# A hybrid decoder step on one core: the gate's sample rows read turned from DRAM, the pool's last rows turned at the end, and another ending for the last two tiles

## The chip, the cores and the metric

The kernel runs on one core of a Trainium2 chip. Its work is issued on five engines with a queue each: TensorE (PE in the profile; PEld are its weight loads), VectorE (DVE), ScalarE (ACT), GpSimd (POOL) and SyncE (SP, which only issues DMAs). The metric is the device time of one execution in microseconds; lower is better.

## The reference, cut to what matters

One layer for a prompt of 1024 tokens and 8 sample tokens, 1024 channels, all in float32:

```python
xn = _rmsnorm(h, pre_g); proj = xn @ w_in
u, v, z_a, x_b, z_b, g_a, g_b = split(proj)
y_a = gelu(u) * spatial_mix(layernorm(gelu(v))) * silu(z_a)
pooled, new_pool = _pool_branch(x_b, prev_pool)     # windows of 2/4/8/16 tokens; new_pool: last 15 rows of x_b
y_b = pooled * silu(z_b)
m = sigmoid(g_a) * (y_a @ w_pa) + sigmoid(g_b) * (y_b @ w_pb)
h = h + _rmsnorm(m @ w_out, post_g)
e = p @ w_ple
gate = sigmoid(_rmsnorm(h, ple_in_g) @ w_pg)
h = h + _rmsnorm(gate * e, ple_out_g)
```

Outputs are `h` of the prompt and of the samples, the normalised `v` of the last chunk, and the pooling rows: the prompt's last 15 rows of `x_b`, and for each sample 14 rows of its old buffer and its new row.

## The kernel before, in words

Prompt and samples stand together as 1032 columns. A product of 1024 x 1024 by 1024 x 1032 is done by pairs of 128 output rows; a pair is one round of Strassen's scheme with seven products, P1 to P7 (`strassen`), each of 12 matmuls of 512 columns or 24 of 260. Each float32 operand is cut into a high and a low part (`split`: a copy on ScalarE, a difference on VectorE) and three of the four cross products are taken, in the form of one pass. A `Step` holds one product: what prepares its weights, the matmuls, and what takes the result out of PSUM; functions are hung behind a step with `at(step, f)`.

The stages in order of time: embedding product and the first branch (to about 400 us), the pooling branch with `XB`, `ZB` and `mixes` (about 360 to 560 us), the second gate, the two merged products, the output product (`Out`, with tokens on partitions) and the gate's product (`Embed`, `gatesteps`, four pairs of token tiles; the last pair holds tiles 6 and 7).

Every instruction is first collected by `Planner.take` with a guessed duration, then `Planner.order` writes out each engine's queue: of what can start, it takes what is due first (`late`, worked back from the uses; a TensorE product is due at its place in the plan's clock, `at`). Loads into the 46 general slots may start some 14 us ahead of their due time. At most eight DMAs of SP and ScalarE are let out at once. The chip then runs these queues as they were written, each engine waiting at the head of its queue. All instructions are issued in `play`, so the profile puts nearly all of them on line 301 and they are told apart by their tiles' names.

Names that the change touches. `XB.tails`: behind a pair of the pooling branch, TensorE turns the last 128 columns of two row blocks into the bank `tail`, ScalarE copies 32 rows of it into `big`, and behind the last pair two DMAs write the pooling outputs. `mixes(g)`: the pooling weights, loaded six steps and cut three steps ahead of their product by the common rule. `sample_stationary`: turns 8 rows into 128-row blocks with eight small transposes (bank `psst`) and VectorE takes them out, with a gain; used for the samples' embedding (`psamp`) and for the samples' rows at the gate (`hs`, in `gate_input(S)`). `sample_rows` and `sample_product`: the samples' product with the raw rows of a weight, four matmuls side by side, bank `sps`. `gated`: sigmoid, product with `e`, sum of squares, and for the last two tiles the product with the gain. `gate_finish`: root of the mean square (VectorE `ms`, GpSimd `rstd`), the scaling, the sum with `h`, the write. For tiles 6 and 7 that sum is one VectorE instruction for each half, with `h` loaded back as `hback`.

The last pair's seven products run in the order `LAST`: P1, P6, P7, P5, P4, P3, P2. P5 and P4 finish tile 7's two halves, P3 tile 6's second half, and P2, in two pieces of 256 columns (`last`), tile 6's first.

Of the kernel before, what the change touches and what calls it, by code (L numbers as in the profile page):

```python
# [19 lines left out]
NS = 8  # L20
# [6 lines left out]
EPS = 1e-6  # L27
POOL_BUF = 15
WINDOWS = (2, 4, 8, 16)
PLE = 256  # L30
# [25 lines left out]
class Planner:  # L56
# [8 lines left out]
    LOAD, LEAD, PATIENCE, RATE, SPARE = 14.0, 14.0, 60.0, 0.36, 3  # L65
    SPARED = 1.0

    def __init__(self, nc, slots, queues):
        self.nc, self.slots, self.queues = nc, slots, queues
        self.ops, self.seen, self.users, self.tags = [], {}, {}, {}  # L70
        self.fixed, self.open, self.clock = True, None, 0.0

        self.loose = set()
        for e in self.ENGINES:
            setattr(self, e, Taker(self, e))
# [54 lines left out]
    def duration(self, engine, method, out, reads, kwargs):  # L130
        n = out.free_size()
        if engine == "tensor":
            if method == "transpose":
                return 0.109
            return 0.3 if "tile_position" in kwargs else max(0.06, 0.0062 + n / 2268)
        if engine == "vector":
# [11 lines left out]
    def take(self, engine, method, args, kwargs):  # L148
# [11 lines left out]
        self.open = (name, op) if engine == "tensor" else None  # L160
        op.calls.append((method, args, kwargs))
        op.spent.append(op.busy)
# [12 lines left out]
        for ap in reads:  # L175
            self.touch(op, ap, False)
        for ap in writes:
            self.touch(op, ap, True)

    def apart(self):  # L180
# [127 lines left out]
def hybrid_step(  # L308
# [519 lines left out]
    def sample_sums(ps):  # L828
# [6 lines left out]
        return parts[2], parts[1]  # L835

    def sample_stationary(src, nk, gain=None):

# [253 lines left out]
    wgcut = {what: dram.tile([HALF, D], F32, tag="wg" + what, name="wg" + what) for what in ('T4', 'B22')}  # L1092
    kept["rowsum"] = dram.tile([NB, P], F32, tag="rowsum", name="rowsum")
    kept["wgleft"] = dram.tile([D, HALF], F32, tag="wgleft", name="wgleft")
# [88 lines left out]

    state_sb, tail = big[:, 7, :D], big[:, 6, :D]
    past = cpool.tile([P, NB, NS], F32, tag="past", name="past")
# [54 lines left out]
    def mixes(g):  # L1240
# [12 lines left out]
        for m in range(2):  # L1253
# [18 lines left out]

            steps.append(Step(nothing if m else prepare, run, evacuate))
        steps[0].loads = loads
        return steps

# [48 lines left out]
    for g, ((w, u), (wz, z)) in enumerate(zip(pairs_of(XB0, XB, "xb"), pairs_of(ZB0, ZB, "zb"))):  # L1325
        bsteps.append((strassen(w, xop, u), strassen(wz, xop, z), mixes(g)))
        xusers.append(u)
# [177 lines left out]
    def out_finish(t):  # L1505
# [6 lines left out]
        dma(kept["h"][t * P : t * P + r, :], h)  # L1512

    rin = lambda t: vsums[: rows(t), t, :1]

# [52 lines left out]
    def ge_start(t):  # L1568
        ge[t], e_of[t], parts[t] = slot("ge", (P, D)), slot("eback", (P, D)), []
        dma(e_of[t][: rows(t)], kept["e"][t * P : t * P + rows(t), :])  # L1570

    def gated(t, c, src):
# [4 lines left out]
        parts[t].append(square_here(g, e_of[t][:r, c]) if len(parts[t]) == 2 else square_sum(g, r))  # L1577
        if len(parts[t]) > 2:
            a, b = parts[t][:2]
            both = sm("both")  # L1580
            nc.vector.tensor_scalar(out=both[:r], in0=a[:r], scalar1=b[:r], scalar2=None, op0=ALU.add)
            parts[t][:2] = [both]
        if NB - 2 <= t < NB:
            mul(g, g, gains["out"][:r, c])

    def gate_finish(t):
        r = rows(t)
        rs = rstd(parts.pop(t), r)
        g = ge.pop(t)
        del e_of[t]  # L1590
        if not NB - 2 <= t < NB:
            g = g[:r]
            nc.vector.scalar_tensor_tensor(out=g, in0=g, scalar=rs[:r], in1=gains["out"][:r],
                                           op0=ALU.mult, op1=ALU.mult)
            nc.gpsimd.dma_start(out=g, in_=kept["h"][t * P : t * P + r, :], accum_op=ALU.add)
            dma(y_of(t), g)
            return
        h = slot("hback", (P, D))
        dma(h, kept["h"][t * P : (t + 1) * P, :])
        for j in range(2):  # L1600
            nc.vector.scalar_tensor_tensor(out=g[:, half(j)], in0=g[:, half(j)], scalar=rs,
                                           in1=h[:, half(j)], op0=ALU.mult, op1=ALU.add)
            dma(y_of(t)[:, half(j)], g[:, half(j)])

    class Embed(User):
        def loads(self):
            for m in range(2):
                ge_start(2 * self.pair + m)

        def direct(self, m, j, ps, c=None):  # L1610
            gated(2 * self.pair + m, c or half(j), ps)

        def summed(self, m, j, ps, u, free=None):
# [3 lines left out]
            gated(t, half(j), o)  # L1617
            if len(parts[t]) == 2:
                gate_finish(t)

        def finish(self):
            for m in range(2):
                if 2 * self.pair + m in ge:
# [299 lines left out]
```

## Time and profile before

| what | value |
|---|---|
| runs | 976.0, 977.59, 977.63 us; median 977.59 |
| profiled execution | 975.89 us, its span 973.8 us |
| granted TensorE clock | 0.997 |
| TensorE busy | 963.8 us, 6077 matmuls |
| VectorE busy | 799.4 us, 1266 instructions |
| ScalarE busy | 532.8 us, 898 instructions |
| GpSimd busy | 68.9 us, 141 instructions |
| DMA | 119308 packets, 185.56 MB |

A timeline row gives the start, the duration, the engine, the line, the operation, output and inputs by their names, the shape and a count. Starts are in us from the beginning of the span. The row of a group gives the shortest, median and longest duration in ns, and the first and last start. A row of windows gives for each engine the busy time in that stretch, then the granted clock, the busy share of the DMA engines and GB/s.

### The profile page before, as it was taken

Reading aid. Unit: us, or ns where it says so; the run is one execution under the profiler, and the core shown is the slowest. Engines: PE = TensorE matmul, PEld = TensorE weight load, DVE = VectorE, ACT = ScalarE, POOL = GpSimd, SP = SyncE. Lnnn points to the kernel's source line nnn. Section 1 sums busy time; section 2 is a strip of 40 time slices with the busy share of each in tenths; the row PEclk is TensorE's granted clock in tenths of the full one; section 3 lists DMA queues with packets and bytes.
Section 4 is the critical chain, followed back from the end, with each engine's and each line's share of the span. In section 5 each row is a group of like instructions: output and inputs, shape, how many; then the busy total and the mean of one; then the engine's idle time right before and its main releaser. Section 6 shows DMA issues by size and latency. Waiting matters only on the chain. (4 is left out here: it accounts for less than half of the span.)

```text
span 973.8 us, 16071 instructions
## 1 busy us (share of the span) xinstructions
PE 963.8 (99%) x6077; PEld 858.9 (88%) x6077; DVE 799.4 (82%) x1266; ACT 532.8 (55%) x898; POOL 68.9 (7%) x141
## 2 busy tenths in 40 slices
PE   9999999999999999999999999999999999999996
PEld 6889999999999999999999999999999986888775
DVE  6997568786889688979897987697699799769786
ACT  7966899865444433344442343552353263977662
POOL 1200000000000000000000100000000001312222
PEclk9999999999999999999999999999999999999998
DMA  9545752532373353666735076884583393799966
GB/s 324 194 130 131 153 153 87 197 104 70 131 281 130 121 185 100 246 218 203 259 122 194 17 257 222 288 301 152 185 294 109 137 339 100 170 280 362 291 187 196
DMA packets 119308, 185.56 MB, mean 191 GB/s; under 512 B 29183, under 2 KB 75735, under 8 KB 119222
## 3 DMA queue, kind: packets, MB, share of 16 engines
q1 hardware_dynamic: 117102, 177.11, 54.1%
q0 software_dynamic: 2080, 7.41, 4.3%
q8 instruction: 48, 0.79, 0.3%
q14 instruction: 30, 0.25, 0.1%
q10 hardware_dynamic: 48, 0.01, 0.0%
HBM read 125.85 MB, written 53.87 MB: 185 GB/s over the span
## 5 line engine op out<-in xcount | busy, mean ns | idle before, releaser
L301 DVE TENSOR_TENSOR u<-acc,u 128x520 f32<-128x520 f32 (+1 forms) x84 | 58.3, 694 | 24.5 <-PE acc L301 22.6
L301 POOL TENSOR_TENSOR rstd<-ms,mhalf 128x1 f32<-128x1 f32 (+1 forms) x36 | 30.4, 885 | 228.2 <-DVE ms L301 196.3
L301 POOL MEMSET u<- 128x8 f32 x32 | 3.3, 104 | 491.1 <-PE acc L301 210.6
L301 ACT ACTIVATE u<-acc 128x512 f32<-128x512 f32 x36 | 21.4, 595 | 23.4 <-PE acc L301 22.7
L301 ACT ACTIVATE paw<-pas 128x512 fp32r<-128x512 f32 x16 | 10.0, 628 | 30.3 <-DVE pas L301 25.1
L301 ACT ACTIVATE pbw<-pbs 128x512 fp32r<-128x512 f32 x16 | 10.0, 628 | 28.9 <-DVE pbs L301 25.7
L301 DVE TENSOR_TENSOR v<-acc,v 128x520 f32<-128x520 f32 (+1 forms) x20 | 13.8, 692 | 12.7 <-PE acc L301 12.6
L301 ACT ACT_TABLE_LOAD x17 | 21.8, 1283 | 4.5 <-PE acc L301 2.0
L301 DVE TENSOR_TENSOR big<-big 128x1024 f32<-128x1024 f32 (+4 forms) x20 | 23.7, 1215 | 0.0
L301 ACT ACTIVATE big<-v 128x1024 uint16<-128x1024 uint16 x16 | 18.6, 1171 | 6.9 <-DMA v<-vw 6.9
L301 PE MATMUL accm<-qh,wpoolw 128*128 128x260 f32 (+1 forms) x96 | 20.9, 320 | 0.0
L301 ACT ACTIVATE zbw<-zbs 128x512 fp32r<-128x512 f32 x16 | 10.0, 627 | 16.5 <-DVE zbs L301 12.3
L301 ACT ACTIVATE big<-mix 128x256 f32<-128x256 f32 x32 | 11.7, 378 | 13.1 <-PE mix L301 12.7
L301 DVE TENSOR_TENSOR acc<-acc,u 128x512 f32<-128x512 f32 (+1 forms) x16 | 11.1, 697 | 8.7 <-PE acc L301 8.7
L301 ACT ACTIVATE gbw<-gbs 128x512 fp32r<-128x512 f32 x16 | 10.0, 626 | 14.8 <-DVE gbs L301 12.6
L301 ACT ACTIVATE uw<-us 128x512 fp32r<-128x512 f32 x16 | 10.0, 627 | 14.0 <-DVE us L301 6.8
L301 PEld LDWEIGHTS accm<-qh,wpoolw 128*128 128x128 f32 x96 | 15.6, 188 | 1.9
L301 ACT ACTIVATE zaw<-zas 128x512 fp32r<-128x512 f32 x16 | 10.1, 629 | 13.1 <-PE acc L301 5.2
L301 DVE TENSOR_TENSOR big<-mix,big 128x256 f32<-128x256 f32 x32 | 12.7, 419 | 5.5 <-ACT big L301 5.3
L301 ACT ACTIVATE vw<-v 128x1024 uint16<-128x1024 uint16 x16 | 16.2, 1044 | 1.8 <-DVE v L301 1.8
L301 ACT ACTIVATE u<-u 128x1032 f32<-128x1032 f32 (+1 forms) x8 | 6.8, 852 | 18.9 <-DVE u L301 18.8
L301 ACT ACTIVATE gb<-gb 128x1032 f32<-128x1032 f32 (+1 forms) x8 | 6.8, 854 | 18.5 <-DVE gb L301 18.5
(668 smaller groups left out, 3593.9 us busy)
## 6 DMA issues: line engine op xcount, KB each, us to landing
ga<-ga SPq DMA_DIRECT2D x16, 516.0 KB
gb<-gb SPq DMA_DIRECT2D x16, 516.0 KB
vraw<-in_w_in_dram SPq DMA_DIRECT2D x22, 256.0 KB
ya<-za SPq DMA_DIRECT2D x8, 516.0 KB
yb<-zb SPq DMA_DIRECT2D x8, 516.0 KB
x<-in_x_prompt_dram SPq DMA_DIRECT2D x8, 512.0 KB
e<-e SPq DMA_DIRECT2D x8, 512.0 KB
garaw<-in_w_in_dram SPq DMA_DIRECT2D x8, 512.0 KB
```

Source lines behind the costliest of these rows:

```text
L301: getattr(getattr(self.nc, e), method)(*args, **kwargs)
```

## The change

Four parts. First, the pooling branch's last columns are no longer turned behind each pair: each row block writes its last 23 columns (15 of the prompt, 8 samples) as they are into a DRAM tensor `ends`; at the end of the kernel one load brings them back, TensorE turns the eight blocks, ScalarE copies two halves out, and two DMAs on ScalarE's queue write the outputs. Second, the samples' rows for the gate are read from DRAM in turned form, element by element, by one DMA on ScalarE's queue; the uses of them move five steps later. Third, the pooling weights' load and cut hang behind fixed steps. Fourth, the ending of tiles 6 and 7: for tile 6's first half, gain times `e` and `e` squared are prepared ahead, so that behind the sigmoid stand a square on ScalarE, a weighted sum on VectorE and one product; its second half gets its gain after the last sum. Tile 7's first half is scaled and added on TensorE (the identity times `h`, a scaled identity times the gate) and copied out and written by ScalarE. The planner gets what it needs for this: a landing time by pieces, a fourfold price for a float32 matmul of 512 columns, and `behind`, which holds an instruction back behind another.

```diff
 class Planner:
-    SPARED = 1.0
+    SPARED, PACKET = 1.0, 0.0025
...
+            if self.packets:
+                op.lands = 2.0 + self.packets * self.PACKET
...
+    def words(out, in_):
+        plan.packets = out.size()
+        dma(out, in_, nc.scalar)
+        plan.packets = 0
...
+    def sample_turned(src, nk, gain=None):
+        turned, st = past.rearrange("p b t -> p (b t)")[:, : NS * nk], twice[:, : nk * NS].rearrange("p (k s) -> p k s", k=nk)
+        words(turned, src.rearrange("s (k p) -> p (s k)", p=P))
+        turned = turned.rearrange("p (s k) -> p k s", k=nk)
...
+            mul(st, turned, gain.unsqueeze(2).to_broadcast([P, nk, NS]))
+        return st
...
         def tails(self):
-            ps = bank("tail")
-            b = 2 * self.pair
             for i in range(2):
-                nc.tensor.transpose(ps[:, i * P : (i + 1) * P], self.out[i][:, T - P : T], ident)
-            nc.scalar.activation(out=tail[96:P, b * P : (b + 2) * P], in_=ps[96:P, : 2 * P], func=AF.Copy)
-            if b == NB - 2:
-                dma(o_pool[0, 0], tail[P - NS - POOL_BUF : P - NS, :])
-                dma(o_spool[0, :, POOL_BUF - 1, :], tail[P - NS : P, :])
+                b = 2 * self.pair + i
+                dma(kept["ends"][b * P : (b + 1) * P, :], self.out[i][:, SEQ - POOL_BUF : T])
...
+        mix, load, prepare = mixes(g)
+        bsteps.append((strassen(w, xop, u), strassen(wz, xop, z), mix))
+        at(bsteps[g][1][1], load)
+        at(bsteps[g][1][5], prepare)
...
         if t == S:
-            samples["h"] = sample_stationary(got, NB, gvec[:, 2 * NB :])
+            samples["h"] = sample_turned(kept["h"][SEQ:T, :], NB, gvec[:, 2 * NB :])
             return
...
+    def gate_ahead():
+        e, c = e_of[END], slice(0, HALF)
+        both = slot("eahead", (P, 2, HALF))
+        mul(both[:, 0], e[:, c], e[:, c])
+        mul(both[:, 1], e[:, c], gains["out"][:, c])
+        ahead["square"], ahead["gain"], ahead["root"] = both[:, 0], both[:, 1], slot("sahead", (P, HALF))
...
+        if t == END and c.start < HALF:
+            s, square = sm("ssq"), ahead["root"][:, c]
+            nc.scalar.activation(out=square, in_=g, func=AF.Square)
+            ahead["squared"] = plan.ops[-1]
+            nc.vector.scalar_tensor_tensor(out=square, in0=square, scalar=1.0 / D, in1=ahead["square"][:, c],
+                                           op0=ALU.mult, op1=ALU.mult, accum_out=s)
+            ahead["summed", c.start] = plan.ops[-1]
+            mul(g, g, ahead["gain"][:, c])
+            ahead["ready", c.start] = plan.ops[-1]
...
+    def last_sum(t, c, rs, h):
+        g = ge[t][:, c]
+        nc.vector.scalar_tensor_tensor(out=g, in0=g, scalar=rs, in1=h[:, c], op0=ALU.mult, op1=ALU.add)
+        dma(y_of(t)[:, c], g)
+
+    def pool_rows():
+        ends, o, ps = slot("ends", (P, NB, ENDS)), slot("rows", (P, D)), region("ends")
+        dma(ends, kept["ends"].rearrange("(b p) t -> p b t", p=P))
+        for b in range(NB):
+            nc.tensor.transpose(ps[:ENDS, b // 4, b % 4 * P : (b % 4 + 1) * P], ends[:, b], ident)
+        plan.ops[-1].at += 8.0
         for j in range(2):
...
+            nc.scalar.activation(out=o[:ENDS, half(j)], in_=ps[:ENDS, j], func=AF.Copy)
+        dma(o_pool[0, 0], o[:POOL_BUF], nc.scalar)
+        dma(o_spool[0, :, POOL_BUF - 1, :], o[POOL_BUF:ENDS], nc.scalar)
+
+    def last_finish():
...
+        t, h = END + 1, hs[END + 1]
+        rs = rstd(parts.pop(t))
+        with plan.behind(ahead["ready", 0]):
+            last_sum(t, half(1), rs, h)
+        scaled, ps, o = slot("scaled", (P, P)), bank("final"), slot("final", (P, HALF))
+        with plan.behind(ahead["squared"]):
+            nc.scalar.activation(out=scaled, in_=ident, func=AF.Copy, scale=rs)
+        for w, x in ((ident, h), (scaled, ge[t])):
+            plan.apart()
+            nc.tensor.matmul(ps, w, x[:, :HALF], start=w is ident, stop=w is scaled)
+            plan.ops[-1].at += 12.0
+        pool_rows()
+        nc.scalar.activation(out=o, in_=ps, func=AF.Copy)
+        dma(y_of(t)[:, :HALF], o, nc.scalar)
+        t, h = END, hs[END]
+        with plan.behind(ahead["summed", QUART]):
+            mul(ge[t][:, half(1)], ge[t][:, half(1)], gains["out"][:, half(1)])
+        rs = rstd(parts.pop(t))
+        for c in (half(1), *CUTS):
+            last_sum(t, c, rs, h)
...
-    at(outsteps[2][3], lambda: gate_input(S))
-    at(gatesteps[0][4], lambda: sample_rows("wg", w_pg, 0))
-    at(gatesteps[1][1], lambda: sample_product("wg", samples["h"], 0))
-    at(gatesteps[1][1], lambda: sample_rows("wg", w_pg, 1))
-    at(gatesteps[1][5], lambda: sample_product("wg", samples["h"], 1))
-    at(gatesteps[1][5], embed_gate_sample)
+    at(gatesteps[0][0], lambda: gate_input(S))
+    at(gatesteps[1][2], lambda: sample_rows("wg", w_pg, 0))
+    at(gatesteps[1][6], lambda: sample_product("wg", samples["h"], 0))
+    at(gatesteps[1][6], lambda: sample_rows("wg", w_pg, 1))
+    at(gatesteps[2][3], lambda: sample_product("wg", samples["h"], 1))
+    at(gatesteps[2][3], embed_gate_sample)
```

More of the change, by code (lines that the diff above doesn't have):

```diff
@@ L161, in take @@
         op.calls.append((method, args, kwargs))
+        if self.first:
+            op.before.add(self.first)
         op.spent.append(op.busy)
@@ L178, in take, with behind @@
             self.touch(op, ap, True)
+    @contextmanager
+    def behind(self, op):
+        self.first = op
+        yield
+        self.first = None
     def apart(self):
@@ L835, in sample_sums @@
         return parts[2], parts[1]
+    def sample_turned(src, nk, gain=None):
+        turned, st = past.rearrange("p b t -> p (b t)")[:, : NS * nk], twice[:, : nk * NS].rearrange("p (k s) -> p k s", k=nk)
+        words(turned, src.rearrange("s (k p) -> p (s k)", p=P))
+        turned = turned.rearrange("p (s k) -> p k s", k=nk)
+        if gain is None:
+            nc.vector.tensor_copy(out=st, in_=turned)
+        else:
+            mul(st, turned, gain.unsqueeze(2).to_broadcast([P, nk, NS]))
+        return st
     def sample_stationary(src, nk, gain=None):
@@ L1271, in evacuate @@
                                                    op0=ALU.mult, op1=ALU.mult)
-            steps.append(Step(nothing if m else prepare, run, evacuate))
-        steps[0].loads = loads
-        return steps
+            steps.append(Step(nothing, run, evacuate))
+        return steps, loads, prepare
     class Merge(User):
@@ L1575, in gated @@
         nc.scalar.activation(out=g, in_=src, func=AF.Sigmoid, scale=rin(t))
-        mul(g, e_of[t][:r, c], g)
[L1577 to L1583, printed above, removed]
+        if t == END and c.start < HALF:
[7 more added lines that the diff above has]
+            ahead["ready", c.start] = plan.ops[-1]
+            parts[t].append(s)
+            if c.start == 0:
+                a, b = parts[t]
+                both = sm("both")
+                nc.vector.tensor_scalar(out=both, in0=a, scalar1=b, scalar2=None, op0=ALU.add)
+                parts[t] = [both]
+            return
+        mul(g, e_of[t][:r, c], g)
+        parts[t].append(square_sum(g, r))
+        if t == NB - 1:
             mul(g, g, gains["out"][:r, c])
@@ L1590, in gate_finish @@
         del e_of[t]
[L1591 to L1599, printed above, removed]
-        for j in range(2):
-            nc.vector.scalar_tensor_tensor(out=g[:, half(j)], in0=g[:, half(j)], scalar=rs,
-                                           in1=h[:, half(j)], op0=ALU.mult, op1=ALU.add)
-            dma(y_of(t)[:, half(j)], g[:, half(j)])
+        g = g[:r]
@@ L1617, in summed @@
             gated(t, half(j), o)
-            if len(parts[t]) == 2:
+            if len(parts[t]) == 2 and t < END:
                 gate_finish(t)
         def finish(self):
+            if self.pair == NPAIR - 1:
+                last_finish()
+                return
             for m in range(2):
```

26 lines of the change are left out of this document (20 added, 6 removed).

## The prediction

> **What bounds the kernel now.** I read the engine totals first, then TensorE's order of time around the transposes that the change touches, then the last ten microseconds engine by engine. In the totals (busy us, share of the span, instructions):
>
> ```profile
> span 973.8 us, 16071 instructions
> PE 963.8 (99%) x6077; PEld 858.9 (88%) x6077; DVE 799.4 (82%) x1266; ACT 532.8 (55%) x898; POOL 68.9 (7%) x141
> ```
>
> TensorE is idle for 10.0 us. The end of the kernel takes 8.4 of them, as the rows below show, so before the last product it hardly ever waits. What leaves TensorE's queue ahead of that product therefore comes off the time, one for one, as long as nothing else becomes late. What leaves VectorE or ScalarE there saves nothing.
>
> TensorE in order of time, at the sample transposes and at the first pair of tail transposes (start, duration, instruction):
>
> ```profile
> 849.14 0.39 PE L301 MATMUL acct<-woT3l,mw 128*128 128x512 f32 x1
> 849.37 0.39 PE L301 MATMUL acct<-woT3h,mw 128*128 128x512 f32 x1
> 849.69 0.66 PE L301 MATMUL psst<-ident,hs 8*128 8x8 f32 x8
> 850.28 0.50 PE L301 MATMUL acct<-woT4h,mw 128*128 128x512 f32 x1
> 850.62 0.39 PE L301 MATMUL acct<-woT4l,mw 128*128 128x512 f32 x1
> ...
> 411.77 0.40 PE L301 MATMUL acc<-xT1l,zbw 128*128 128x260 f32 x2
> 412.01 0.40 PE L301 MATMUL acc<-xT1h,zbw 128*128 128x260 f32 x2
> 412.25 0.38 PE L301 MATMUL tail<-ident,xb 128*128 128x128 f32 x2
> 412.39 0.48 PE L301 MATMUL acc<-xB11h,xbw 128*128 128x512 f32 x1
> 412.71 0.39 PE L301 MATMUL acc<-xB11l,xbw 128*128 128x512 f32 x1
> ...
> L301 PE MATMUL tail<-ident,xb x8: 270/272/273, 412.3 to 549.1; 128*128 128x128 f32 x8
> ```
>
> Durations overlap, so the price of a group is the distance of starts across it, less the usual distances. Then the end: the last matmul, VectorE's, ScalarE's, GpSimd's and the DMA queue's rows, and the DMA traffic of the last stretch in 40 slices.
>
> ```profile
> 965.11 0.28 PE L301 MATMUL last<-wgB21h,hw 128*128 128x256 f32 x1
> ...
> 964.10 1.03 DVE L301 TENSOR_TENSOR ge<-eback,ge 128x512 f32<-128x512 f32 x2
> 965.05 1.41 DVE L301 SCALAR_TENSOR_TENSOR ge<-ge,rstd,hback 128x512 f32<-128x512 f32 x2
> 966.37 0.42 DVE L301 TENSOR_TENSOR ge<-eback,ge 128x256 f32<-128x256 f32 x1
> 966.83 0.42 DVE L301 SCALAR_TENSOR_TENSOR eback<-ge 128x256 f32<-128x256 f32 x1
> 967.42 0.21 DVE L301 TENSOR_SCALAR ms<-both,ssq 128x1 f32<-128x1 f32 x1
> 967.55 1.35 DVE L301 TENSOR_TENSOR ge<-ge,out 128x512 f32<-128x512 f32 x3
> 968.99 1.42 DVE L301 SCALAR_TENSOR_TENSOR ge<-ge,rstd,hback 128x512 f32<-128x512 f32 x2
> ...
> 964.83 0.63 ACT L301 ACTIVATE junk<-ge 128x512 bf16<-128x512 f32 x1 [0.33 <-DVE ge L301]
> 965.46 0.45 ACT L301 ACTIVATE ge<-last,vsums 128x256 f32<-128x256 f32 x1
> 965.82 0.40 ACT L301 ACTIVATE junk<-ge 128x256 bf16<-128x256 f32 x1
> ...
> 967.71 0.93 POOL L301 TENSOR_TENSOR rstd<-ms,mhalf 128x1 f32<-128x1 f32 x1 [3.26 <-DVE ms L301]
> ...
> 969.77 1.00 SPq L301 DMA_DIRECT2D out_dram<-ge  x2
> 970.43 0.33 SPq L301 DMA_DIRECT2D out_dram<-ge  x1
> ...
> DMA  0000439796969698999899999898989898988210
> DMA packets 287, 0.52 MB, mean 308 GB/s; under 512 B 31, under 2 KB 31, under 8 KB 287
> ```
>
> Call the end of the last matmul E: 965.11 + 0.28 = 965.39. The span ends at E+8.4. VectorE works without a gap from E−0.3 to E+5.0: it scales tile 7 (965.05), then does tile 6's last quarter, the sum of squares, three gain products, and the last scaling. The two last writes (0.52 MB) are issued at E+4.4 and E+5.0; the DMA slices (970.4 to 972.1, 0.0425 us each) show traffic from about E+5.2 to E+6.6 at full share, some 360 GB/s. The last 1.8 us belong to the writes' completion.
>
> **The change part by part.** *Sample transposes out.* From 849.37 to 850.62 two matmuls and the eight transposes pass: 1.25 us. Two usual steps are 2 × 0.23 (849.14 to 849.37), so the group costs 0.79 us, and all of it goes. The turned read on ScalarE's queue replaces it; it has no TensorE part, and the VectorE product with the gain stays.
>
> *Tail transposes moved.* From 412.01 to 412.71 is 0.70 us; without the pair it would be 0.24 + 0.23. A pair costs 0.23, the four pairs (x8 in the group) 0.92 us. They come back as eight transposes after E, where TensorE has 8.4 idle us. Four ScalarE copies, which were off the path, become two at the end. Eight small column writes, a load, and two output writes replace two writes. The small writes go to SP's queue in the pooling stage, at the price of an issue there (0.33 us in the row of 970.43), eight times; nobody waits for them until the end.
>
> *The turned read itself: 8192 pieces of 4 bytes.* The nearest row is the early load of the spatial weights' first entries, 1024 pieces of 4 bytes (128 partitions × 8); a bulk transpose, 2048 pieces of 256 bytes, is the other end. DMA traffic of 22 to 25 us, where those 4-byte pieces land:
>
> ```profile
> L301 SPq DMA_DIRECT2D w<-in_w_s_dram x1: 378/378/378, 17.7 to 17.7; - x1
> L301 SPq DMA_TRANSPOSE v<-vw x8: 1919/2132/3654, 80.6 to 130.9; - x8
> DMA packets 1330, 1.10 MB, mean 366 GB/s; under 512 B 1082, under 2 KB 1090, under 8 KB 1321
> ...
> 889.20:893.60 4.40, 4.40 (x20) 3.57 (x19) 4.01 (x9) 0.06 (x2) 1.47 (x3) 1.00 1.08 351
> 890.00:900.00 10.00, 10.00 (x45) 8.14 (x44) 9.08 (x16) 4.48 (x8) 2.34 (x3) 1.00 1.06 326
> 940.00:950.00 10.00, 10.00 (x57) 8.65 (x56) 9.53 (x16) 6.72 (x14) 3.21 (x3) 1.00 0.58 131
> 950.00:960.00 10.00, 10.00 (x45) 8.13 (x44) 5.58 (x10) 2.41 (x7) 3.74 (x4) 1.00 0.92 237
> ```
>
> Its landing: 1024 pieces within those 3 us beside other traffic, so 8192 take up to 24 us. It is asked for after the gate's first step, and its first use now stands after the second pair's last step: 13 steps of 2.8 us (twelve matmuls at 0.23), 36 us later. Hidden. Its issue on ScalarE: between 0.4 us (the 4-byte row) and 2.13/2048 × 8192 = 8.5 us (the transpose's rate). I take 0.4 to 1, by the row of the same form. ScalarE is idle for 4.3 us at 889 (window row: ACT 0.06 of 4.40), so up to about 4 us are covered. The upper end is a rival below. Its traffic meets a DMA share of 1.06, but the sample's eight row loads leave that stretch, being asked for five steps later.
>
> The Trainium skill's page "DMA: Bandwidth & Descriptors", section "Rules for kernel authors", speaks against this edit: a strided last dimension becomes one descriptor per element and should be rearranged. By the page the read is slow; by these rows slow is affordable, so the sum keeps zero.
>
> *Sample product and gate later; pool weights earlier; gains multiplied ahead.* The same instructions move by five steps; the two new VectorE products (two of about 0.68, the size of the 128x512 products above) land in 940 to 960, where VectorE has 0.5 + 4.4 us free in 20. Without that cover they cost 1.4 us. The pool weights' load and split move up by two or three steps: zero while slots last.
>
> *The new end.* Tile 6's chain after the last quarter's sigmoid is now a square on ScalarE, a sum on VectorE, and the root. ScalarE: square of half 1 to E+0.1, sigmoid E+0.1, square E+0.45 to 0.85. VectorE: sum of quarter 0 and its product (2 × 0.42) to E+0.4, tile 7's second half (0.7) to E+1.2, sum of quarter 1 to E+1.6, `ms` to E+1.8 (before: E+2.2), root 0.93 to E+2.8, the two remaining products (0.68 + 0.42) beside it, then scalings of 0.75, 0.42 and 0.42 to E+4.35. Before it was E+5.0, so VectorE gains 0.65.
>
> Tile 7's first half goes another way: two full-precision matmuls of 512 columns, each two instructions at a distance of about 0.41 us by the sample products' rows, which have the same form:
>
> ```profile
> L301 PE MATMUL sps<-wgrows,sst x32: 592/592/596, 914.0 to 931.2; 128*8 128x512 f32 x32
> ```
>
> (592 against 390 ns for one pass of 0.23: 0.2 more, so 0.41 to 0.43 each.) First matmul to E+0.7, eight transposes to E+1.6, second matmul to E+2.5, ScalarE's copies to E+3.4, then its write is issued, with data from E+4.2.
>
> But the bytes at the end grow. Before, 0.52 MB flowed after E+5.2. Now 256 KB of tile 7, 512 KB of tile 6 and 92 KB of pool rows, 0.88 MB, all follow E+4.2: at 360 GB/s 2.4 us, to E+6.6, exactly where the data end today. VectorE's 0.65 us are then eaten by the writes. Bounds: +0.8 us gain (the writes don't bind; a 128 KB last write instead of 256), −0.5 us (tile 7's write starts after tile 6's). I take a gain of 0.1.
>
> The page named above, section "Issuing engines are not separate DMA queues", says the same of ScalarE's queue: another queue saves issue time, no bandwidth. No row of this kernel shows both queues loaded at once; if they were separate, the gain here would be 0.65.
>
> *Sum:* 0.79 + 0.92 + 0.1 = 1.8 us. The profiled execution took 975.89 us (span 973.8 and 2.1 around it), so it would take 974.1. It stands 1.7 below the median of 977.59, beside the lowest run (976.0). Carried to the median: 975.8.
>
> **Rivals.** *The end pays in full.* For it: the last write is half as large and is issued 0.65 us earlier. Against: 0.88 MB at 360 GB/s. Gain 1.71 + 0.8 = 2.5: 975.1.
>
> *The pool's transposes don't go last.* The planner gives them a time 8 us after TensorE's last planned one, but its operands are there early, and a matmul that isn't ready lets them slip ahead of the last product. They cost 0.9 there; gain 0.9: 976.7.
>
> *The sample's late product meets the last pair's banks.* Product, its emptying, and the last pair's first product:
>
> ```profile
> 929.88 1.90 PE L301 MATMUL sps<-wgrows,sst 128*8 128x512 f32 x16
> 933.74 0.68 DVE L301 TENSOR_TENSOR slow<-sps,slow 8x512 f32<-8x512 f32 x1
> 945.66 0.28 PE L301 MATMUL last<-wgB11h,hw 128*128 128x256 f32 x1
> ```
>
> Its bank is free at 934.4, 11 us before the last pair's first product asks for one of the same two banks. Moved by five steps (14 us) that room is gone, unless its loads, asked for at a time of less traffic, let it follow its place in the plan more closely. Against: the planner can let other products pass. A wait of 1.5 us: 977.3.
>
> *Slower: the turned read blocks ScalarE.* One mechanism: the issue takes the transpose's rate, 8.5 us, in ScalarE's queue in the first gate pairs. Behind it stand the splits of the next weights and the emptying of TensorE's accumulators. Idle time covers 4.3 us, and the remaining 4.2 us are late for TensorE. It decides from 4.3 + 1.8 = 6.1 us of issue. Time 975.8 + 4.2 = 980.0, or 978 at 6.5 us of issue. For it: the only instruction here with thousands of pieces takes 2 us and more. Against: 1024 pieces of this form take 0.38 us.
>
> **How the numbers follow.** Forecast 0.50; end in full 0.17; transposes ahead 0.11; banks 0.09; slower 0.13. A measurement of this kernel can tell about 0.2%, 2.0 us, from no change. The forecast's gain of 1.8 lies just under that, and its own range (1.3 to 2.3) on both sides: of its 0.50 I put 0.23 to faster, 0.27 to same. Faster: 0.23 + 0.17 = 0.40, and 0.02 of the runs' own scatter: 0.42. Same: 0.27 + 0.11 + 0.07 = 0.45, less that 0.02: 0.43. Slower: 0.13 + 0.02 = 0.15. The range runs from 973.5 (gain of 2.5 from the lowest run, 976.0) to 978.0 (ScalarE blocked for 6.5 us); beyond lie some 0.15 above and 0.05 below.
>
> **What would show it.** TensorE: no `psst` from the gate's samples and no `tail` among the products, and its last product ends 1.7 us earlier, near 963.7. If it ends later than 964.5, a stall is there, and the idle time before a matmul names it. ScalarE's queue: one DMA of 32 KB in the gate stage, under 1 us long; if several us, the slower rival. The end: last data about 6.6 us after E; if 5.9, the end pays in full. Eight transposes of `ends` after the last `last` product; if ahead of it, the second rival.

## The result, and the profile after

The changed kernel takes 982.90 us (median of 6), the kernel before 976.12 us on the same chip: a ratio of 1.0067, 95% interval 1.0058 to 1.0077. By that ratio it is 6.5 us slower. The forecast was 975.8, within 973.5 to 978.0. The profiled execution took 983.75 us with a span of 982.0.

The totals of the changed kernel:

```profile
span 982.0 us, 16100 instructions
PE 967.2 (98%) x6073; PEld 860.4 (88%) x6073; DVE 798.7 (81%) x1268; ACT 532.3 (54%) x898; POOL 69.3 (7%) x141
```

Its waits by cause, of TensorE, then the one that is new on VectorE, then SyncE's for the turned read (us in total, times, longest):

```profile
PE acct L315 <- DVE ge L315: 4.0, 1, 4.0
PE accm L315 <- ACT xb L315: 1.3, 1, 1.3
...
DVE hs L315 <- DMA out_dram<-ge: 6.6, 1, 6.6
...
SPq L315 <- DMA past<-h: 12.2, 1, 12.2
```

TensorE does not do more: 6073 matmuls against 6077. Two waits stand in it that the kernel before has not: 1.3 us at 473, for `xb`, and 4.0 us at 919. The rows around the longer one (ScalarE's and SyncE's DMA issues, VectorE, TensorE):

```profile
887.46 0.41 ACTq L315 DMA_DIRECT2D past<-h  x1
...
904.72 2.54 SPq L315 DMA_DIRECT2D wgrows<-in_w_pg_dram  x2
919.51 1.25 SPq L315 DMA_DIRECT2D out_dram<-ge  x2
...
914.96 0.69 DVE L315 TENSOR_TENSOR hw<-big,hw 128x512 fp32r<-128x512 f32 x1
922.27 0.69 DVE L315 TENSOR_TENSOR hs<-big,hs 128x512 f32<-128x512 f32 x1 [6.62 <-DMA out_dram<-ge]
...
919.19 0.40 PE L315 MATMUL acct<-wgT4h,hw 128*128 128x512 f32 x1
923.62 0.50 PE L315 MATMUL acct<-wgB22h,hw 128*128 128x512 f32 x1 [4.04 <-DVE ge L315]
```

Three windows there, with the granted clock in the third column from the end:

```profile
916.00:919.00 3.00, 3.00 (x15) 2.44 (x14) 0.00 (x0) 0.00 (x0) 0.00 (x0) 1.00 0.79 137
919.00:923.60 4.60, 0.58 (x3) 0.15 (x1) 1.32 (x3) 0.00 (x0) 0.00 (x0) 1.00 0.71 251
923.60:928.00 4.40, 4.38 (x13) 3.44 (x14) 3.34 (x6) 2.82 (x6) 0.00 (x0) 0.64 0.25 101
```

VectorE wants a slot for `hs`, and by the releaser in its row the slot it is given is the one of a finished tile's `ge`, whose write to the output is asked for only at 919.51. TensorE, which waits for VectorE, stands for 4.0 us, and then runs at a granted clock of 0.64 for 4.4 us (13 matmuls where 19 of 0.23 us would start: 1.4 us more). In the kernel before, the same VectorE instruction takes a slot that the samples' product has just given back:

```profile
913.97 1.90 PE L301 MATMUL sps<-wgrows,sst 128*8 128x512 f32 x16
915.92 0.69 DVE L301 TENSOR_TENSOR hs<-big,hs 128x512 f32<-128x512 f32 x1 [0.39 <-PE sps L301]
```

The end of the changed kernel (TensorE; VectorE's last sums; then SyncE's last issues and GpSimd's last accumulating transfer into `ge`), and the last two such transfers of the kernel before:

```profile
970.95 0.28 PE L315 MATMUL last<-wgB21h,hw 128*128 128x256 f32 x1
971.07 1.04 PE L315 MATMUL ends<-ident,ends 128*23 128x128 f32 x8
971.94 1.02 PE L315 MATMUL final<-hback,ident 128*128 128x512 f32 x2
972.94 1.12 PE L315 MATMUL final<-ge,scaled 128*128 128x512 f32 x2
...
974.36 1.54 DVE L315 SCALAR_TENSOR_TENSOR ge<-ge,rstd,hback 128x512 f32<-128x512 f32 x3
...
944.34 8.83 SPq L315 DMA_DIRECT2D eback<-e  x4
969.02 9.64 SPq L315 DMA_DIRECT2D out_dram<-ge  x6
...
966.75 0.89 POOL L315 DMA_DIRECT2D ge<-h  x1 [1.95 <-issue]
```

```profile
953.15 0.87 POOL L301 DMA_DIRECT2D ge<-h  x1 [0.30 <-DMA out_dram<-ge]
954.86 0.86 POOL L301 DMA_DIRECT2D ge<-h  x1 [0.84 <-DVE ge L301]
```

E, the end of the last product, is at 970.95 + 0.28 = 971.23 instead of 965.39 (+5.8); from E to the end of the span it takes 10.8 us instead of 8.4 (+2.4). The tiles before the last two now finish 12 us later than before (966.75 against 954.86), so that their writes stand in SyncE's queue among the last writes. SyncE is through with its last write at 978.66 (969.02 + 9.64), 2.8 us after VectorE's last sum (975.90).

### The profile page after: what moved, and what is told of

Its sections match the earlier page's. It is cut to its first block, busy times and chain, and to the rows that moved or that the text cites. A ratio compares the mean times of both kernels' runs of the same rounds, so it can differ in the third digit from the quotient of the medians.

```text
span 982.0 us, 16100 instructions
## 1 busy us (share of the span) xinstructions
PE 967.2 (98%) x6073; PEld 860.4 (88%) x6073; DVE 798.7 (81%) x1268; ACT 532.3 (54%) x898; POOL 69.3 (7%) x141
## 5 line engine op out<-in xcount | busy, mean ns | idle before, releaser
L315 ACT ACTIVATE ge<-ge,vsums 128x512 f32<-128x512 f32 x12 | 8.6, 717 | 16.1 <-DVE ge L315 16.1
```

What stands on the lines that cost most here:

```text
L315: getattr(getattr(self.nc, e), method)(*args, **kwargs)
```

## The experiments

In each table row below, E and "end" (from E to the end of the span) are those of the profiled execution, which for e14 is its longest, 980.8 us; ratios are against the kernel before on the same chip. "Old steps" are the places of the six sample steps before the change.

| run | median us | ratio, 95% interval | E | end |
|---|---|---|---|---|
| before | 976.1 | 1 | 965.4 | 8.4 |
| after | 982.9 | 1.0067 (1.0058 to 1.0077) | 971.2 | 10.8 |
| e1: after without the sample part | 977.1 | 1.0013 (1.0004 to 1.0023) | 967.1 | 8.9 |
| e2: before with the sample part alone | 981.6 | 1.0053 (1.0035 to 1.0071) | 969.8 | 9.4 |
| e3: after, read in 256-byte pieces | 981.8 | 1.0058 (1.0041 to 1.0075) | 969.5 | 10.8 |
| e4: after, no read, later steps | 983.0 | 1.0077 (1.0062 to 1.0092) | 968.4 | 12.7 |
| e5: before with the read, old steps | 982.1 | 1.0062 (1.0044 to 1.0080) | 971.6 | 8.3 |
| e6: before with the pool rows at the end | 976.2 | 0.9999 (0.9990 to 1.0008) | 966.1 | 8.2 |
| e7: before with earlier pool weights | 979.8 | 1.0033 (1.0020 to 1.0045) | 969.4 | 8.8 |
| e8: before with the new end | 975.5 | 0.9992 (0.9983 to 1.0001) | 965.0 | 8.2 |
| e9: e5, read in 256-byte pieces | 981.9 | 1.0061 (1.0045 to 1.0077) | 971.5 | 8.4 |
| e10: e5, read on GpSimd's queue | 1016.0 | 1.0409 (1.0392 to 1.0425) | 1004.9 | 9.0 |
| e11: e4, two weight rows at a time | 980.2 | 1.0045 (1.0030 to 1.0060) | 968.3 | 9.4 |
| e12: e6 and e8 together | 977.8 | 1.0016 (1.0006 to 1.0025) | 966.9 | 8.6 |
| e13: e5, planned as if the read landed at once | 991.1 | 1.0152 (1.0135 to 1.0169) | 978.3 | 11.4 |
| e14: e13, read in 256-byte pieces | 976.7 | 1.0020 (1.0006 to 1.0033) | 967.4 | 11.6 |
| e15: after, planned as if the read landed at once | 993.0 | 1.0173 (1.0158 to 1.0188) | 980.8 | 10.7 |
| e16: before with the later steps alone | 980.0 | 1.0046 (1.0031 to 1.0061) | 968.3 | 9.9 |
| e17: e8, two weight rows at a time, old steps | 975.6 | 0.9995 (0.9986 to 1.0003) | 965.7 | 8.0 |
| e18: e8 again, more runs | 975.5 | 0.9992 (0.9983 to 1.0001) | 965.3 | 8.2 |

**Which part.** My first theory after the result (A) was the slow landing of the turned read: at most eight DMAs of ScalarE and SyncE are let out at once, so the eighth behind the read, which is the output write at 919.51, has to wait for it (SyncE's 12.2 us above). The rivals: the steps' later places (B), the new end and the pool rows (C).

e1, the sample part undone:

```diff
-            samples["h"] = sample_turned(kept["h"][SEQ:T, :], NB, gvec[:, 2 * NB :])
+            samples["h"] = sample_stationary(got, NB, gvec[:, 2 * NB :])
...
-    at(gatesteps[0][0], lambda: gate_input(S))
-    at(gatesteps[1][2], lambda: sample_rows("wg", w_pg, 0))
+    at(outsteps[2][3], lambda: gate_input(S))
+    at(gatesteps[0][4], lambda: sample_rows("wg", w_pg, 0))
...
```

> The changed kernel with the sample part undone: the gate's sample rows are turned on TensorE again and the six steps stand where they stood; the pool rows at the end, the earlier pool weights and the new end stay. Theory A (the turned read of 8192 four-byte pieces lands after 32 us, and SP's queue waits for it at the eighth DMA behind it): the wait of 4.0 us on VectorE near 919 and the half-clock stretch behind it are gone, about 6.6 us, so about 976 us; the 1.3 us wait at 472 stays, as it comes from the weights' earlier load. Rival B (the moved steps, not the read, bring the samples' work too late): the same 976 here, told apart by the run with the steps alone. Rival C (the loss comes from the new end and the pool rows): 981 or more here.

e2 is the other half: the kernel before with these lines of the change and no other.

> The kernel before with the sample part alone: the turned read and the six moved steps, no other edit. Theory A: the stall near 919 is there in full, 6 to 7 us, less 0.8 us of transposes: about 982 us. Rival B: the same. Rival C (the new end and the pool rows make the loss): 975 to 976 us.

e1 gives 1.0013 and e2 1.0053: 1.3 and 5.2 us, which add up to the whole 6.5. So C falls as the main cause, and most of the loss is in the sample part. e3 and e4 split it.

```diff
-        words(turned, src.rearrange("s (k p) -> p (s k)", p=P))
+        words(turned, src.rearrange("s (q f) -> (s q) f", f=NS * nk))
```

> The changed kernel with one DMA's pattern altered: the same 32 KB of the samples' rows are read as 128 pieces of 256 bytes instead of 8192 of 4 bytes, on the same queue at the same place, so every engine's order stays the same; the turn itself is left out, so the samples' gate is computed from wrongly arranged values. Theory A: the read lands within about 3 us, SP's queue has no hole between 907 and 919, PE's wait of 4.0 us and the half-clock stretch go: E (end of the last product) at about 964.6 instead of 971.2, the whole 974 to 977 us. Rival B (late steps): nothing changes, 982 to 983 us. Rival C (new end): nothing changes, 982 to 983 us.

e4 has only the first line of the diff of e1 (the transposes come back), and leaves the steps at their later places.

> The changed kernel with the samples' rows turned on TensorE as before, but with the six steps at their new, later places. Theory A: no stall near 919; the eight-column transposes cost their 0.8 us again: about 976.5 us. Rival B (the steps' later places make the stall): 981 to 983 us. Rival C (new end): 982 us or more.

Here theory A fell as the main cause: with pieces of 256 bytes only 1 us comes back (981.8), and with no read at all nothing does (983.0). It keeps a share. The same rows of e3 (SyncE, VectorE, TensorE's longest wait):

```profile
916.07 3.47 SPq L315 DMA_DIRECT2D out_dram<-ge  x2
...
920.54 0.69 DVE L315 TENSOR_TENSOR hs<-big,hs 128x512 f32<-128x512 f32 x1 [4.52 <-DMA out_dram<-ge]
...
PE acct L315 <- DVE ge L315: 1.9, 1, 1.9
```

TensorE's longest wait at this place is 4.0 us in the changed kernel and 3.5 in e2, which have the slow read, and 1.9, 1.6 and 2.0 in e3, e4 and e16, which have not. So about half of it is the read's, though e4 loses as much again at its end (12.7 us); the other half is there without the read. e16, with the later steps alone, is the kernel before with the six lines of `at`:

> The kernel before with the six sample steps at their later places and nothing else: TensorE turns the rows, no read, the old end and pool rows. Theory D: 980 to 983 us, with a wait on VectorE near 919 and the loads of e for the last tiles after 943. Theory K: 975.5 to 977 us.

It costs 4.5 us. Its rows show the same slot wait and the same late ending as those of the changed kernel (VectorE, TensorE, SyncE, GpSimd):

```profile
920.75 0.69 DVE L315 TENSOR_TENSOR ge<-acct,u 128x512 f32<-128x512 f32 x1 [4.40 <-DMA out_dram<-ge]
...
921.50 0.50 PE L315 MATMUL acct<-wgB22h,hw 128*128 128x512 f32 x1 [1.98 <-DVE ge L315]
...
930.06 1.90 PE L315 MATMUL sps<-wgrows,sst 128*8 128x512 f32 x16
...
944.50 3.16 SPq L315 DMA_DIRECT2D eback<-e  x4
...
964.92 0.92 POOL L315 DMA_DIRECT2D ge<-h  x1 [1.95 <-issue]
```

The samples' first product stands at 930 instead of 914, so its four weight rows give their slots back 16 us later; VectorE at 916 gets a slot behind an output write. The loads of `e` for the last tiles wait the same way (944.50; the kernel before has three of them at 934.99), and the tiles end late.

**Is it the slots?** e11 takes e4 and halves what the samples' product holds: four parts of two weight rows, at steps spread over the same stretch.

```diff
     def sample_rows(key, src, b):
-        rawrows[key, b] = [slot(f"{key}rows", (P, D)) for _ in range(4)]
+        n = 2 if key == "wg" else 4
+        rawrows[key, b] = [slot(f"{key}rows", (P, D)) for _ in range(n)]
...
+    at(gatesteps[1][4], lambda: sample_product("wg", samples["h"], 0))
+    at(gatesteps[1][4], lambda: sample_rows("wg", w_pg, 1))
+    at(gatesteps[1][6], lambda: sample_product("wg", samples["h"], 1))
...
```

> The run with the moved steps alone (983.0 us, transposes on TensorE), with the sample product cut into four parts of two weight rows instead of two of four: the same loads, products and last step, but two slots held at a time instead of four. Theory D (slots: the weight rows hold four slots while the gate's tiles wait for theirs): the wait on the output write near 919 and the late loads of e at 943 are eased, 978 to 980 us. Theory J (the samples' late gate itself makes the loss, whatever its slots): 982 to 983 us.

980.2 against 983.0: 2.8 us come back with the same loads, the same products and the same last step, all of it in the end (9.4 us instead of 12.7; E is the same). The wait near 919 is gone, and one of 1.2 us stands at 945 instead. The weight rows' slots are thereby a cause, though the four parts also stand at other steps, so some of the 2.8 us may be the order's. The 4.4 us that remain against the kernel before are not split further.

**What the read costs.** e5 is the kernel before with the read, steps at their old places; e9 is e5 with the edit of e3.

> The kernel before with the turned read in place of the eight TensorE transposes, and nothing else: the six sample steps stand where they stood. Theory D (the later steps make the loss: the weight rows of the sample product keep their slots while the gate's tiles ask for slots, and the read is nearly free): 0.8 us of transposes go, the stall near 919 is absent, so about 975.0 us against 975.8. Theory A (the slow landing holds SP's queue at the eighth DMA behind it): a wait of 1 to 4 us appears some 30 us behind the read's issue, 977 us or more.

> The kernel before with the read in place of the transposes and the steps where they stood, but the 32 KB are read as 128 pieces of 256 bytes instead of 8192 of 4 bytes; the turn is left out, so the samples' gate is computed from wrongly arranged values. Every engine's order is that of the run with the turned read at the old steps (982.1 us). Theory A2 (there the slow landing alone makes the loss: SP's queue stands still from 872 to 881 until the read has landed): the hole and PE's wait of 2.2 us at 892 go, and 0.8 us of transposes are saved: about 975 us. Theory G (the other order that the planner writes once the read is in it makes the loss): 980 to 982 us again.

Both lose 6 us, so at first the landing seemed not to matter here either. But both run one order, and the planner had written it counting on a landing of 22 us. SyncE's queue in e5, then in e9:

```profile
871.34 0.33 SPq L315 DMA_DIRECT2D h<-h  x1
881.64 0.87 SPq L315 DMA_DIRECT2D wgT<-wghigh  x2
```

```profile
872.08 0.33 SPq L315 DMA_DIRECT2D h<-h  x1
874.94 0.93 SPq L315 DMA_DIRECT2D wgT<-wghigh  x2
```

In e5 the queue stands for 10 us, in e9 for 3; but ScalarE and VectorE cut these weights at the same late place of their queues, and TensorE's longest wait is the same in both, e5 and e9:

```profile
PE acct L315 <- DVE wgT3l L315: 2.2, 1, 2.2
```

So e13, e14 and e15 change the planner's price, 0.0025 us for a piece:

```diff
-    SPARED, PACKET = 1.0, 0.0025
+    SPARED, PACKET = 1.0, 0.0
```

> The kernel before with the turned read at the old steps (982.1 us), but the planner's price of a 4-byte piece set to zero, so that it counts on a landing of 2 us. Theory K (the planned order makes the loss there: the planner holds the weights' loads behind the read and puts other work ahead of their splits): 975 to 976.5 us. Theory A (the real landing holds SP's queue, whatever was planned): 980 us or more, and SP's queue with a hole from about 872 on.

> The same order as the run before it, with 128 pieces of 256 bytes in place of 8192 of 4 (the turn is left out, so the samples' gate is computed from wrongly arranged values). Theories A and K both: about 975 us, the price of the transposes (0.8 us) below the kernel before. What the run before it takes over this one is the real landing. Theory G (any new order costs some us): 978 us or more.

> The changed kernel (982.9 us) with the planner's price of a 4-byte piece set to zero. Theory D (the steps' later places and their slots make most of the loss): 981 to 983 us. Theory K: 976 to 978 us.

e13 and e14 have the same order on every engine and differ by the pieces alone: 991.1 and 976.7, 14 us (13 by the ratios). e9 and e14 differ by the planner's price alone: 981.9 and 976.7, so the order written for a slow read costs 4 to 5 us even where the read lands early. e13 in order of time (VectorE, TensorE):

```profile
880.32 0.27 DVE L315 TENSOR_TENSOR twice<-past,gvec 128x64 f32<-128x64 f32 x1 [15.03 <-DMA past<-h]
...
881.24 0.80 PE L315 MATMUL acct<-woT4h,mw 128*128 128x512 f32 x1 [9.27 <-DVE u L315]
```

Its DMA queues from 860 to 877, then from 877 to 880.2 (q1 is SyncE's, q10 ScalarE's; packets, MB, share):

```profile
q1 hardware_dynamic: 1899, 4.41, 73.5%
q10 hardware_dynamic: 4454, 0.02, 15.0%
...
q10 hardware_dynamic: 3754, 0.02, 67.2%
q1 hardware_dynamic: 96, 0.16, 13.4%
```

The first use stands at the head of VectorE's queue for 15 us, and TensorE behind it for 9.3. The read, asked for at 860.1, needs 20 us: beside SyncE's packets 4454 pieces pass in 17 us, almost alone 3754 in 3.2. e15, the changed kernel in an order that does not count on the slow read, gets to 993.0 with the same row (VectorE held for 12.07 us by `past<-h`). So the planner's price of a piece turns a loss of 14.8 us (e13) into one of 6.1 (e5), and with the later steps into one of 5.2 (e2). And in e14, with a read that lands at once and no transposes, the kernel is still not faster than before (of its ten runs five lie between 975.3 and 976.2, the others reach up to 980.8).

e10 took the read off the queue that SyncE waits for: 16 DMAs of 512 pieces on GpSimd's.

```diff
+        for s in range(NS):
+            for k in range(0, nk, 4):
+                words(turned[:, s * nk + k : s * nk + k + 4],
+                      src[s : s + 1, k * P : (k + 4) * P].rearrange("s (k p) -> p (s k)", p=P))
...
-        dma(out, in_, nc.scalar)
+        dma(out, in_, nc.gpsimd)
```

> The kernel before with the turned read at the old steps, asked for on GpSimd's queue in 16 parts of 512 pieces of 4 bytes, whose landing SP's queue does not wait for. Theory A2: no hole in SP's queue near 872 to 881; 975 to 977 us, the upper end if GpSimd's issues delay its accumulating transfers. Theory H (the 8192 pieces cost by the DMA engines' time, whichever queue asks): 979 us or more.

It missed by 40 us. The group of these DMAs on GpSimd (busy, mean ns; idle before them):

```profile
L315 POOL DMA_DIRECT2D past<-h x16 | 12.3, 767 | 50.5 <-issue 38.8 <-DVE ms L315 5.5 <-DVE wgT3l L315 4.7
```

TensorE's longest waits there:

```profile
PE acct L315 <- DVE u L315: 16.6, 2, 16.1
PE pht L315 <- DMA h<-in_x_prompt_dram: 8.3, 1, 8.3
```

GpSimd stands 39 us without a cause that the profile shows before these 16 issues, and its own work, the roots and the accumulating loads of `h`, waits behind them.

**The other three parts.** Each alone on the kernel before: e6 the pool rows (the hunks of `tails`, `ends` and `pool_rows`), e7 the early pool weights, e8 the new end (`gate_ahead`, `gated`, `last_finish`); e12 is e6 and e8 together. Besides those hunks, e6 needs the first of these edits, e8 the second, and the third is e7, for which `mixes` returns its load and its cut:

```diff
         def finish(self):
+            if self.pair == NPAIR - 1:
+                pool_rows()
...
     def last_finish():
...
-        pool_rows()
...
-        bsteps.append((strassen(w, xop, u), strassen(wz, xop, z), mixes(g)))
+        mix, load, prepare = mixes(g)
+        bsteps.append((strassen(w, xop, u), strassen(wz, xop, z), mix))
+        at(bsteps[g][1][1], load)
+        at(bsteps[g][1][5], prepare)
```

> The kernel before with the pool's last rows alone moved to the end: eight small writes of columns, one load, eight transposes after the last product, two output writes; the end of the last two tiles, the pool weights' load and the samples stay. Theory D: 0.9 us less before the last product (E at 964.5 instead of 965.4), the end 0 to 0.5 us longer, so 975.0 to 975.5 us. Rival E (the eight writes in SP's queue delay the loads behind them and make the wait of 1.3 us at 472): the wait is there and the time is 976.5 us.

> The kernel before with the pool weights' load and split alone put earlier. Theory D: this brings the wait of 1.3 to 1.6 us at 472, so about 977.2 us. Rival E (the eight small writes make it): no wait, 975.8 us.

> The kernel before with the new end of the last two tiles alone (tile 7's first half through TensorE, tile 6's products ahead); the pool rows are turned and written where they were. Theory D: E stays at 965.4, the end takes 8.0 to 8.9 us (8.4 before), so 975.4 to 976.3 us. Rival F (the new end is the loss of the run without the sample part, 2.3 us against the 0.9 us gained by the pool rows): 977 us or more.

> The kernel before with the pool rows at the end and the new end of the last two tiles, without the sample part and without the earlier pool weights. Theory: the new end alone gave 975.5 and the pool rows alone 976.2, against 976.1 before; if the earlier pool weights are what the run with all but the sample part (977.1) loses, this gives 975.0 to 976.0 us; if the two ends disturb each other, 977 us.

e6 gains nothing: the 0.9 us of transposes are gone, and a new wait of 1.0 us stands in their place. VectorE's low part `ql` of the pooled rows waits for a write of the gate's weights, and TensorE for `ql` (e6 in order of time); in the kernel before, `ql` starts at 467.39 with no wait:

```profile
469.73 1.23 DVE L315 TENSOR_TENSOR ql<-big,qh 128x1032 fp32r<-128x1032 f32 x1 [1.81 <-DMA wglow<-wgraw]
...
471.02 0.50 PE L315 MATMUL accm<-ql,wpoolw 128*128 128x512 f32 x1 [0.99 <-DVE ql L315]
```

```profile
467.39 1.23 DVE L301 TENSOR_TENSOR ql<-big,qh 128x1032 fp32r<-128x1032 f32 x1
```

e7 has the wait on `xb` at 473 (1.2 us) that the changed kernel has, and one of 0.9 us on `zb`, and costs 3.2 us. Yet e12, the pool rows and the new end alone, is not faster than e1, which has the early weights besides (977.8 and 977.1): the parts do not add up, since every edit makes the planner write another order from there on. e8 is 0.8 us under the kernel before, with an interval that reaches 1.0001. The last two runs asked whether it is a gain, and whether two weight rows at a time (the edit of e11, from `gatesteps[0][4]` to `gatesteps[1][5]`) add to it:

> The new end of the last two tiles alone again, with more rounds: 975.2 to 975.8 us against 975.6 to 976.1 before, a ratio of 0.9990 to 0.9996 whose interval should end below 1.0 if the gain is real.

> The kernel before with the new end of the last two tiles and, at the steps' old places, the sample product in four parts of two weight rows. If slots bind there too: some tenths to 1 us below the new end alone, 974.5 to 975.3 us. If they bind only at the late places: equal to the new end alone, 975.5 us, or above it where the planner's order comes out worse (976 to 978).

Neither can be told from no change: e18 repeats the ratio of e8, 0.9992, and its interval again reaches 1.0001, so a gain of 0.8 us is suggested twice and not shown; e17 adds nothing to it. No version is shown to beat the kernel before.

## Why the prediction was wrong

By parts, the sum had a gain of 0.79 us for the sample part, which costs 5.2 (e2), and a gain of 1.0 us for the tail transposes and the new end; these two and the early pool weights together cost 1.3 (e1). Its base, the median of 977.59, was that of three runs and lay 1.5 us above the 976.12 measured beside the changed kernel; from there the same sum would have read 974.3, further off.

**Failed, the largest: "Sample product and gate later".** The step counted the moved instructions, "the same instructions move by five steps", and asked only what VectorE's two new products cost. The steps alone cost 4.5 us (e16). What was left out is what the moved loads hold: four slots of 46, which in the kernel before come back when the product begun at 913.97 ends, and VectorE, already waiting, takes one at 915.92 (the row with `<-PE sps`). The prediction wrote "zero while slots last" for the pool weights and did not ask it of the samples' rows. The rival of the late samples' product named the wrong resource (banks) and 1.5 us.

**Failed: "The turned read itself ... Hidden".** The landing was put at up to 24 us, from 1024 pieces in 3 us. Those pieces ran in the same queue as the packets beside them (SyncE's, 366 GB/s); here they stood in a second queue, and in full stretches passed only one for one with SyncE's packets (last section). From 887.46 to 919.51, when the write behind it is let out, it is 32 us. The cover was counted to the first use alone, 36 us later; the first to wait is the eighth DMA behind the read. The limit of eight was known from the kernel, and the step did not use it. Its price in the changed kernel is small, since the order allows for it: e3 gives 1 us back. Against the transposes that it replaces, the read comes out 0.7 us dearer by e2 less e16 and 1.0 us cheaper by the changed kernel less e4; neither is clear of the intervals. In an order that does not allow for it, it costs 13 to 14 us (e13 less e14).

The Trainium skill's page "DMA: Bandwidth & Descriptors", section "Rules for kernel authors", which the prediction weighed and set aside, holds: the 32 KB came as 8192 pieces, and two runs that differ in nothing else are 13 to 14 us apart.

**Right: no long issue on ScalarE.** The read is issued in 0.41 us, as the row of the same form said. So the slower rival named the right side and the wrong mechanism, and its sign (an issue of several us) is absent.

**Right in size, lost again: the tail transposes, 0.92 us.** They are gone, but alone they give 0.1 us (e6), because the new order makes TensorE wait 1.0 us at 470. "What leaves TensorE's queue ahead of that product therefore comes off the time, one for one" came with the condition "as long as nothing else becomes late", and the sum did not ask after it: in e6 VectorE's `ql` became late.

**Right: the new end, 0.1 us.** In e8 and in e18 the end takes 8.2 us instead of 8.4. In the changed kernel it takes 10.8, since the earlier tiles' writes arrive late in the same queue; the step had assumed that only the last two tiles write there.

**Wrong: pool weights "zero while slots last".** 3.2 us alone (e7); with the pool rows and the new end beside them, nothing (e1 against e12).

**The signs.** `tail` and the `psst` of the gate's samples are absent among the products, the eight transposes of `ends` stand behind the last `last` product, so the second rival is out. E at 971.23 instead of 963.7 was the sign for a stall, and the idle time before the matmul at 923.62 named VectorE's `ge`, and VectorE's row the write.

## What to carry to other kernels

A transfer that moves in time takes its buffers with it: before pricing it at zero, look up which instruction takes the buffer next and who releases it, in the row of its wait. A read of thousands of small pieces is priced by the DMAs that may not pass it and by the traffic beside it, not by its own issue or by its first use. Where a planner rewrites the whole order after each edit, 1 us saved on the busiest engine is within what the new order may lose, so each part is to be timed alone.

## What the runs showed that was not expected

**Small pieces beside large packets.** In e13, 4454 pieces of 4 bytes passed in 17 us beside 1899 packets of SyncE's queue (262 in a us), and 3754 in 3.2 us almost alone (1170 in a us). The 17 us are not even. In stretches that SyncE's packets fill, the two counts come out equal; where they leave the DMA engines idle, many more pieces pass. Two full stretches, in e13 from 870 to 874 (174 pieces in a us) and in the changed kernel from 897 to 899 (125 in a us):

```profile
q1 hardware_dynamic: 699, 1.36, 91.3%
q10 hardware_dynamic: 697, 0.00, 10.4%
```

```profile
q1 hardware_dynamic: 250, 0.80, 98.5%
q10 hardware_dynamic: 250, 0.00, 7.1%
```

The Trainium skill's page "DMA: Bandwidth & Descriptors", section "Queues, rings and completion order", says that a DMA engine takes turns between queues by packets of some 9 to 17 descriptors. Equal counts fit turns of equal length from both queues; they do not show how long a turn is, and no run tested it.

**The clock after a wait.** The granted clock fell to about 0.6 after waits of 4.0 us (the changed kernel) and of 1.9 us (e3), and stayed at 1.00 after one of 2.0 us (e16), in the window behind each:

```profile
921.50:926.00 4.50, 4.11 (x11) 3.25 (x12) 3.71 (x7) 2.58 (x5) 0.00 (x0) 0.62 0.35 117
```

```profile
921.50:926.00 4.50, 4.50 (x19) 3.68 (x20) 2.96 (x5) 2.76 (x6) 0.00 (x0) 1.00 0.81 245
```

The Trainium skill's page "TensorE: Matmul & The Clock Gate", section "HAM oscillation — how this bites in real kernels", gives as the rule no idle gaps above some 3.4 us. The row of e3 has a drop after a gap of about half that, so a short wait can cost twice: 1.9 us of standing, and then 11 matmuls started in a window where e16 starts 19 (0.4 us of e3's window still belongs to the wait). What decides between 1.9 and 2.0 us was not tried.
